# Earlier requests for plain weight tiles, and gate blocks read during convolution output

## The chip, the cores and the metric

One NeuronCore of a Trainium2 chip runs the whole layer in one launch. The metric is the device time in microseconds, as the median of several runs, beside one execution taken by the hardware profiler.

## The reference

One block of a language model on 512 positions of width 1024, in float32: half a feed-forward layer, a mixer, half a feed-forward layer, each on an RMS-normalized input and added to it, and a last normalization.

```python
for l in range(DEPTH):                                  # DEPTH = 1
    x = x + 0.5 * swiglu(rmsnorm(x, norm_ffn1_g[l]), ffn1_w_gu[l], ffn1_w_down[l])
    x = x + hybrid_mixer(rmsnorm(x, norm_mix_g[l]), w_in[l], ...)
    x = x + 0.5 * swiglu(rmsnorm(x, norm_ffn2_g[l]), ffn2_w_gu[l], ffn2_w_down[l])
return rmsnorm(x, final_norm_g)

def hybrid_mixer(h, w_in, conv_w, ..., w_out_conv, w_out_gla, w_o):
    cb, cc, cu, q, k, v, g_lr, r, ga, gb = split(h @ w_in)
    y_conv = (cb * causal_short_conv(cc * cu, conv_w)) @ w_out_conv
    o = gated_linear_attention(q, k, v, decay(g_lr))    # 4 heads, chunks of 64
    y_gla = (normalized(o) * silu(r)) @ w_out_gla
    return (sigmoid(ga) * y_conv + sigmoid(gb) * y_gla) @ w_o
```

The change concerns `sigmoid(gb) * y_gla`, with `y_conv` just ahead of it, and the order in which weights are fetched.

## The kernel before, in words

**Layout.** Activations lie transposed, features on the 128 partitions, positions along the row: a tile of 128 x 512 is one block of features. Each float32 operand is split into a high part (`h`, a copy by ScalarE, L310) and a low part (`l`, a subtraction by VectorE, L311), and a product is three matmuls.

**Plain tiles and sets of block products.** All weight units are listed in `PLAN`, and the order in which TensorE takes them in `STEPS`. An entry is either plain (`p` is None: one weight tile and its matmuls, 24 of them with 512 columns) or one of the seven products of a set (`m1`, `p2`, `q6`, `p5`, `q7`, `p4`, `p3`), by which a 2 x 2 block product takes seven block multiplications instead of eight. One such step is 24 matmuls with 256 columns (L502); ScalarE copies the results of `m1`, `q6` and `q7` out of PSUM (L507), and the next product into that bank waits for the copy. A set takes five tiles of the ring `f`: four weight blocks, which SP's queue reads, and a sum; four more sums are formed in place by accumulating DMAs that POOL issues (L288).

**The order of the stages.** First feed-forward: plain tiles, sets, then the plain tiles of the down projection. Mixer: plain tiles for attention's inputs, then twelve sets (`MSETS`: gates `ga` and `gb`, convolution, `r`), with attention's heads woven between them; then convolution output (`w_out_conv`, eight plain tiles, about 719 to 763 us in the profile); then attention output (`w_out_gla`, two sets, 763 to 807 us); then `w_o`, plain. Second feed-forward: plain tiles, sets, sets of another shape (`wide_sets`), and the last plain tiles.

**Who asks for weights.** `Weights.take` issues the split of the step two ahead. `issue` first calls `fetch`, which asks for the plain tiles among the next `early` steps (5 in the feed-forward layers, 4 in the mixer) and stops at the first set step; the blocks of a set are asked for six steps before its `m1`. All of these are reads of 512 KB into the ring `f` of ten tiles, on SP's queue (L284).

**Gates.** The `ga` and `gb` blocks of the mixer's input product go to DRAM when they are made. `gate(name, d, l, t)` reads a block back (L1307 for a whole tile of `ga`, L1309 for a half of two tiles of `gb`, 256 KB either way) and applies the sigmoid in place (ScalarE, L1311). Convolution output reads one `ga` tile for each of its eight tiles. Attention output reads four `gb` blocks for each of its sets, inside `gla_done`, into four work tiles of attention, `E`, `M`, `KS` and `EX`; both sets use these tiles. `E`, `M`, `KS` and `QS` are also used in convolution output's first four tiles, to spread the norms of the four heads (L1330, L1333). `vt[1]` are four tiles of the same shape that hold the values `v` of heads 2 and 3.

**What sets the order.** The text gives each instruction a priority; the framework's planner orders the instructions of each engine and queue with it, by its own estimate of durations, and starts an instruction ahead of others when its inputs and its tile are free. Tiles of a ring are given out in the order of the text. On the chip each queue then runs in that fixed order and waits for what isn't ready.

Of the kernel before, what the change touches and what calls it, by code (L numbers as in the profile page):

```python
# [102 lines left out]
STEPS = []  # L103
# [81 lines left out]
def block_kernel(ctx: ExitStack, tc: tile.TileContext, xT, vecs, gf, gup, wgl, wts, out):  # L185
# [21 lines left out]
    def tile_of(pool, shape, dtype=F32):  # L207
        cnt[0] += 1
        return pools[pool].tile(shape, dtype, tag=pool, name=f"{pool}{cnt[0]}")

    def T(dtype=F32):
        return tile_of("tp", [P, S], dtype)
# [31 lines left out]
    class Weights:  # L244
# [26 lines left out]
        def fetch(self, at):  # L271

            for n, p in STEPS[at : min(at + self.early, self.end)]:
                if p is None and n not in self.raw:
                    self.raw[n] = self.dma(n)
                elif p is not None:
                    break

        def dma(self, n):
# [62 lines left out]
    def mm_single(mat, kt, col, ah, al):  # L342
        o = MM()
        for u in single(mat, kt, col):
            h, l = W.take(u)
            for i in range(u[2]):
                k = u[1] + i
                mm3(o, h[:, i * P : (i + 1) * P], l[:, i * P : (i + 1) * P],
                    ah[k], al[k], k == 0, k == kt - 1)
        return o  # L350
# [124 lines left out]
    def mul(out_, a, b, eng=None):  # L475
        (eng or nc.vector).tensor_tensor(out=out_, in0=a, in1=b, op=ALU.mult)
# [390 lines left out]
    def mixer(norm, nxt):  # L867
# [13 lines left out]
        def two(i):  # L881
            return flat(i).rearrange("p (e t) -> p e t", e=2)
# [3 lines left out]
        vt = [[V0[t // 2][:, t % 2] for t in range(NTB)],  # L886
              [tile_of("v", [P, S]) for _ in range(NTB)]]

        def G_tile(i, dtype=F32):
            cnt[0] += 1  # L890
            return pools["g"].tile([P, S], dtype, tag=f"g{i}", name=f"g{i}_{cnt[0]}")
# [93 lines left out]
        E, M, KS, EX, QS = (G_tile(i) for i in range(5))  # L985
# [180 lines left out]
        def pair(t):  # L1166
            return t.rearrange("p (e t) -> p e t", t=HW)

        def half(l):
            return slice(l * HW, (l + 1) * HW)  # L1170
# [19 lines left out]
        def finish_late():  # L1190
            while late:
                late.pop(0)()
# [38 lines left out]
        def quarter(s, p):  # L1231

            bank, v = s.bank, s.v
            if p not in ("p2", "q7", "p3"):
                return None
            t = T()
            if p == "q7":
                nc.vector.scalar_tensor_tensor(out=t, in0=bank["c"], scalar=-1.0, in1=v["q7"],  # L1238
                                               op0=ALU.mult, op1=ALU.subtract)
            else:  # L1240
                nc.vector.tensor_tensor(out=t, in0=bank["a" if p == "p2" else "c"],
                                        in1=v["m1" if p == "p2" else "q6"], op=ALU.add)
            return t
# [49 lines left out]
        def split_pair(v):  # L1293
            h, l = (tile_of("op", [P, 2, S], F32R) for _ in range(2))
            nc.scalar.copy(h, v)
            nc.vector.tensor_tensor(out=l, in0=v, in1=h.bitcast(F32), op=ALU.subtract)
            return [(h[:, i], l[:, i]) for i in range(2)]
# [5 lines left out]
        def gate(name, d, l=None, t=None):  # L1303

            t = T() if t is None else t
            if l is None:
                nc.sync.dma_start(t, gates_d[name][d])  # L1307
            else:
                nc.sync.dma_start(pair(t), gates_d[name][d : d + 2, :, half(l)].rearrange(  # L1309
                    "e p t -> p e t"))  # L1310
            nc.scalar.activation(t, t, AF.Sigmoid)  # L1311
            return t
# [8 lines left out]
        Of = OB[0].rearrange("p h e t -> p (h e) t")  # L1321
        oo = Operands(lambda j, l: Of[:, 4 * j : 4 * j + 4, half(l)])
        AT = {3: "m1", 4: "p2", 6: "p5"}
        for d in range(KD):
            t = gate("ga", d)
            yp = mm_single("w_out_conv", KD, d * P, c_h, c_l)
            mul(m[d], yp, t)
            if d < HEADS:
                tr, orow = (E, M) if d % 2 else (KS, QS)
                nc.vector.tensor_copy(  # L1330
                    tr.rearrange("p (b c) -> p b c", c=32),
                    r64[:, 16 * d : 16 * (d + 1)].unsqueeze(2).to_broadcast([P, 16, 32]))
                nc.vector.transpose(orow, tr)  # L1333
                mul(O[d], O[d], orow.unsqueeze(1).to_broadcast([P, 2, S]))
            if d in AT:
                oo.make(AT[d])
        oo.sum("q6")
        m_h, m_l = [None] * KD, [None] * KD

        def gla_done(i):  # L1340
            sg = {}

            def done(s, p):
                if not (i == 1 and p in ("q6", "p5", "q7")):
                    finish_late()
                if p == "m1":
                    sg[0, 0] = gate("gb", 4 * i, 0, E)
                if p == "p5":
                    sg[1, 1] = gate("gb", 4 * i + 2, 1, M)
                    sg[1, 0] = gate("gb", 4 * i + 2, 0, KS)  # L1350
                if p == "p4":
                    sg[0, 1] = gate("gb", 4 * i, 1, EX)
                if p not in ("p2", "q7", "p4", "p3"):
                    return
                a, l = int(p in ("p4", "q7")), int(p in ("q7", "p3"))
                d = 4 * i + 2 * a
                g = sg[a, l]
                if p == "p4":
                    nc.vector.scalar_tensor_tensor(out=g, in0=s.bank["b"], scalar=-1.0, in1=g,
                                                   op0=ALU.mult, op1=ALU.mult)  # L1360
                else:
                    mul(g, quarter(s, p), g)
                y = two(d // 2)
                nc.vector.tensor_tensor(out=y[:, :, half(l)], in0=y[:, :, half(l)], in1=pair(g),
                                        op=ALU.add)
                if p in ("p4", "p3"):
                    def f():
                        for j, (b, c) in enumerate(split_pair(y)):
                            m_h[d + j], m_l[d + j] = b, c
                    late.append(f)  # L1370
            return done

        def reload():
            XS.append(big("X2"))
            x[:] = [XS[-1][:, k] for k in range(KD)]
            for k in range(KD):
                nc.gpsimd.dma_start(x[k], xs[k])

        run_sets(lambda i: Set(oo, gla_done(i)), hooks={(0, "p3"): [reload]})
        finish_late()  # L1380

# [24 lines left out]
    with phase("small2", f=10, tp=6, v=4, qk=2, g=1, y=4, small=1):  # L1406
        W.phase(4, 5)
        n2 = Norm(V_G2)
        mixer(nm, n2)
# [46 lines left out]
```

## Time and profile before

| | us |
|---|---|
| median of 3 runs | 1209.31 (1205.89 to 1211.93) |
| profiled execution | 1207.32 |
| its span, first to last instruction | 1205.6 |
| TensorE busy in it | 1187.8 (99%) |
| VectorE, ScalarE, POOL busy | 840.7, 612.1, 130.0 |
| read from HBM, written to it | 124.55 MB, 8.39 MB |

In rows of a timeline stand the start and the duration in us, the engine, the line, the operation and its tiles (out<-in), and in brackets the idle time of the engine before it with what ended it. In rows of waits stand the total, how often, and the longest. In rows of windows stand the stretch, its length, and for each engine the busy time with the count, then the granted TensorE clock, the share of the DMA engines and GB/s. In rows of the chain stand start, duration and what the end of the program hung on at that time.

### The profile page before, as it was taken

The numbers are of one execution on the slowest core, as the hardware profiler recorded it, in microseconds if no ns is written. First come the engines' busy times: TensorE is split into PE (matmuls) and PEld (weight loads), VectorE is DVE, ScalarE is ACT, GpSimd is POOL, SyncE is SP. The second block draws the span as 40 slices with busy tenths as digits, with TensorE's granted clock in tenths as the row PEclk, the third lists the DMA queues.
The fourth block names the chain that finished last, engine by engine and source line by source line (L and its number), as shares of the span: only waits on it lengthen the run. The fifth ranks groups of instructions, "written<-read, shape, count | busy, mean of one in ns | idle before, by whom it ended". The sixth has DMA issues, their size and how long they took to land.

```text
span 1205.6 us, 19145 instructions
## 1 busy us (share of the span) xinstructions
PE 1187.8 (99%) x7834; PEld 1092.1 (91%) x7834; DVE 840.7 (70%) x990; ACT 612.1 (51%) x762; POOL 130.0 (11%) x155
## 2 busy tenths in 40 slices
PE   9999999999999999999999999999999999999987
PEld 8899999988888889999999998898889999997776
DVE  7976666732277765868688687586597656589865
ACT  6555455532254465646554575454355455466453
POOL 0011111000010001101011100200001111113420
PEclk9999999999999999999999999999999999999999
DMA  9477777531162325767777756752447777757711
GB/s 349 95 200 189 178 187 186 167 105 53 52 241 92 88 70 150 213 171 186 194 184 176 192 182 183 208 149 93 161 99 194 189 175 177 183 143 197 161 50 70
DMA packets 59496, 190.81 MB, mean 158 GB/s; under 512 B 6576, under 2 KB 12848, under 8 KB 59408
## 3 DMA queue, kind: packets, MB, share of 16 engines
q1 hardware_dynamic: 37936, 124.27, 29.6%
q0 software_dynamic: 16832, 60.83, 27.3%
q10 hardware_dynamic: 4640, 4.49, 1.2%
q8 instruction: 61, 1.00, 0.3%
q14 instruction: 27, 0.22, 0.1%
HBM read 124.55 MB, written 8.39 MB: 110 GB/s over the span
## 4 chain that ended last, share of the span: by engine, by line
PE 89%; DVE 4%; DMA 3%; issue 2%; ACT 1%; POOL 0%; SPq 0%; DVEq 0%; ACTq 0%; POOLq 0%
PE mm L502 50%; PE mm L362 7%; PE mm L340 6%; PE mm L338 6%; PE mm L339 6%; DVE wl L311 2%; DMA f<-f 1%; PE mm L380 1%; PE mm L381 1%; PE mm L379 1%; DMA g<-gb 1%; DMA f<-wts 1%; PE aux L340 1%; PE aux L338 1%; PE aux L339 1%
## 5 line engine op out<-in xcount | busy, mean ns | idle before, releaser
L502 PE MATMUL mm<-op,wh 128*128 128x256 f32 x3584 | 649.9, 284 | 3.3 <-ACT tp L507 3.3
L310 ACT CAST wh<-f 128x1024 fp32r<-128x1024 f32 (+1 forms) x325 | 339.6, 1046 | 483.6 <-PE mm L502 225.2
L311 DVE TENSOR_TENSOR wl<-f,wh 128x1024 fp32r<-128x1024 f32 (+1 forms) x325 | 400.4, 1235 | 242.0 <-ACT wh L310 230.2
L502 PEld LDWEIGHTS mm<-op,wh 128*128 128x128 f32 x3584 | 560.2, 192 | 4.9 <-ACT tp L507 3.9
L502 PE MATMUL mm<-op,wl 128*128 128x256 f32 x1792 | 507.9, 284 | 0.0
L502 PEld LDWEIGHTS mm<-op,wl 128*128 128x128 f32 x1792 | 344.0, 192 | 0.1
L288 POOL DMA_DIRECT2D f<-f x108 | 93.3, 869 | 847.0 <-DVE wl L311 470.1
L340 PE MATMUL mm<-op,wl 128*128 128x512 f32 x324 | 126.4, 390 | 0.1
L338 PE MATMUL mm<-op,wh 128*128 128x512 f32 x324 | 126.5, 390 | 0.0
L339 PE MATMUL mm<-op,wh 128*128 128x512 f32 x324 | 126.1, 389 | 0.0
L340 PEld LDWEIGHTS mm<-op,wl 128*128 128x128 f32 x324 | 60.8, 188 | 13.2 <-DVE wl L311 0.5
L339 PEld LDWEIGHTS mm<-op,wh 128*128 128x128 f32 x324 | 60.8, 188 | 12.6
L338 PEld LDWEIGHTS mm<-op,wh 128*128 128x128 f32 x324 | 60.8, 188 | 12.4
L362 PE MATMUL mm<-op,wh 128*128 128x512 f32 x256 | 63.5, 390 | 0.3 <-DVE op L413 0.3
L362 PEld LDWEIGHTS mm<-op,wh 128*128 128x128 f32 x256 | 47.9, 188 | 10.6 <-ACT acc L422 0.4
L507 ACT COPY tp<-mm 128x512 f32<-128x512 f32 x96 | 55.8, 581 | 1.2 <-DVE tp L1238 1.0
L747 PE MATMUL mm<-wh,op 128*128 128x512 f32 x112 | 44.4, 398 | 4.1 <-ACT wh L310 2.4
L749 PE MATMUL mm<-wl,op 128*128 128x512 f32 x112 | 45.0, 401 | 2.1 <-DVE wl L311 2.0
L297 DVE TENSOR_TENSOR f<-f,f 128x1024 f32<-128x1024 f32 x36 | 44.0, 1221 | 1.8 <-DMA f<-f 1.0
L751 PE MATMUL mm<-wh,op 128*128 128x512 f32 x112 | 44.2, 395 | 0.0
L551 DVE TENSOR_TENSOR op<-hidw,op 128x1024 fp32r<-128x1024 f32 x28 | 36.0, 1297 | 1.3 <-ACT op L550 1.3
L550 ACT CAST op<-hidw 128x1024 fp32r<-128x1024 f32 x28 | 29.1, 1047 | 11.0 <-DVE hidw L597 4.0
(270 smaller groups left out, 1157.6 us busy)
## 6 DMA issues: line engine op xcount, KB each, us to landing
f<-wts SPq DMA_DIRECT2D x219, 512.0 KB, 4.3
f<-f POOLq DMA_DIRECT2D x108, 512.0 KB, 5.0
X<-xT SPq DMA_DIRECT2D x8, 256.0 KB, 4.9
xs<-X POOLq DMA_DIRECT2D x8, 256.0 KB, 5.4
ga<-tp ACTq DMA_DIRECT2D x8, 256.0 KB, 3.9
gb<-tp ACTq DMA_DIRECT2D x8, 256.0 KB, 4.1
g<-gb SPq DMA_DIRECT2D x8, 256.0 KB, 3.8
tp<-ga SPq DMA_DIRECT2D x8, 256.0 KB, 4.8
```

The source lines that it names most:

```text
L288: nc.gpsimd.dma_start(out_, a, accum_op=ALU.add)
L310: nc.scalar.copy(h[:, :w], raw[:, :w])
L311: nc.vector.tensor_tensor(out=l[:, :w], in0=raw[:, :w], in1=h[:, :w].bitcast(F32), op=ALU.subtract)
L338: nc.tensor.matmul(o, wh, ah, start=first, stop=False)
L339: nc.tensor.matmul(o, wh, al, start=False, stop=False)
L340: nc.tensor.matmul(o, wl, ah, start=False, stop=last)
L362: nc.tensor.matmul(o[c], w[:, s : s + P], a[k], start=k == 0 and j == 0, stop=k == kt - 1 and j == 2)
L502: nc.tensor.matmul(to, ww[:, s], aa[:, t], start=fresh and k == 0 and e == 0 and j == 0, stop=k == 3 and j == 2, skip_group_check=True)
L507: nc.scalar.copy(v, o)
L747: nc.tensor.matmul(o[t], bh[:, s], wh, start=fresh and k == 0, stop=False, skip_group_check=True)
L749: nc.tensor.matmul(o[t], bh[:, s], wl, start=False, stop=False, skip_group_check=True)
L751: nc.tensor.matmul(o[t], bl[:, s], wh, start=False, stop=k == 3, skip_group_check=True)
```

## The change

Two edits. In `fetch`, the search for plain tiles no longer stops at a set step when the step being issued is itself one of a set: it passes over the rest of the set and asks for the plain tiles behind it, up to `early` steps ahead. Where the step being issued is plain, it stops as before.

In the mixer, the eight `gb` reads and sigmoids leave `gla_done`. `early_gate` is called once for each tile of convolution output: for tiles 0 to 3 it reads set 0's four blocks into the tiles `vt[1]`, for tiles 4 to 7 set 1's four into `E`, `M`, `KS` and `EX`. `gla_done` takes them from the table `gb`.

```diff
@@ fetch
                 if p is None and n not in self.raw:
                     self.raw[n] = self.dma(n)
-                elif p is not None:
+                elif p is not None and STEPS[at][1] is None:
                     break
@@ mixer
         AT = {3: "m1", 4: "p2", 6: "p5"}
+        gb = {}
+
+        def early_gate(i, a, l, t):
+            gb[i, a, l] = gate("gb", 4 * i + 2 * a, l, t)
+
         for d in range(KD):
             t = gate("ga", d)
             yp = mm_single("w_out_conv", KD, d * P, c_h, c_l)
...
             if d in AT:
                 oo.make(AT[d])
+            if d < 4:
+                early_gate(0, d % 2, d // 2, vt[1][d])
+            else:
+                early_gate(1, d % 2, (d - 4) // 2, (E, M, KS, EX)[d - 4])
...
         def gla_done(i):
-            sg = {}
-
             def done(s, p):
                 if not (i == 1 and p in ("q6", "p5", "q7")):
                     finish_late()
-                if p == "m1":
-                    sg[0, 0] = gate("gb", 4 * i, 0, E)
-                if p == "p5":
-                    sg[1, 1] = gate("gb", 4 * i + 2, 1, M)
-                    sg[1, 0] = gate("gb", 4 * i + 2, 0, KS)
-                if p == "p4":
-                    sg[0, 1] = gate("gb", 4 * i, 1, EX)
                 if p not in ("p2", "q7", "p4", "p3"):
                     return
                 a, l = int(p in ("p4", "q7")), int(p in ("q7", "p3"))
                 d = 4 * i + 2 * a
-                g = sg[a, l]
+                g = gb[i, a, l]
```

## The prediction

> **What bounds the kernel now.** I read the page first, then who waits for whom on TensorE, then the chain of waits around the two stages that the change touches, then the timelines there.
>
> ```profile
> span 1205.6 us, 19145 instructions
> PE 1187.8 (99%) x7834; PEld 1092.1 (91%) x7834; DVE 840.7 (70%) x990; ACT 612.1 (51%) x762; POOL 130.0 (11%) x155
> PE mm L502 <- ACT tp L507: 3.3, 3, 1.8
> PE mm L747 <- ACT wh L310: 2.4, 1, 2.4
> PE mm L749 <- DVE wl L311: 2.0, 4, 0.9
> ```
>
> TensorE is busy for 1187.8 of 1205.6 us, so 17.8 us is all that a better order of transfers could give, and some of that is the start and the end. The waits of TensorE say where the rest lies: 3.3 us in the block products (L502) for ScalarE's copy out of PSUM (L507), and 4.4 us in the last stage (L747, L749). The chain shows what stands behind the first of these.
>
> ```profile
> 762.96 5.77 PE mm L502 x48
> ...
> 771.37 0.61 DVE y L1364
> ...
> 772.00 7.88 DMA g<-gb
> ...
> 781.52 0.49 ACT tp L507
> ...
> 782.06 24.79 PE mm L502 x192
> 806.85 0.23 PE mm L362
> 779.96 0.63 ACT L1311 ACTIVATE g<-g 128x512 f32<-128x512 f32 x1 [4.53 <-DMA g<-gb]
> 782.65 1.05 ACT L310 CAST wh<-f 128x1024 fp32r<-128x1024 f32 x1 [0.65 <-DMA f<-f]
> 782.06 0.50 PE L502 MATMUL mm<-op,wh 128*128 128x256 f32 x2 [1.84 <-ACT tp L507]
> 894.41 25.92 PE mm L502 x216
> ```
>
> This is attention output (762.96 to 806.85). Tile E serves both sets of products: set 0's use ends at 771.98 (L1364), only then may set 1's gate block be read into it, and the read takes 7.88 us. ScalarE works in order; the sigmoid (L1311) stands at the head of its queue and holds it for 4.53 us, with a weight split (L310) and the copy L507 behind it. TensorE needs that copy and stands idle for 1.84 us.
>
> **The change, part by part.**
>
> *Gate blocks read earlier.* It removes all eight reads and sigmoids from the block products of attention output and puts them into the loop of convolution output, one per tile. Set 0's four go to the V tiles, set 1's to E, M, KS, EX, so no read waits for the other set's use any more. The stage holds 14 steps of 24 products. Undisturbed, a product takes 25.92 / 216 = 0.120 us (row at 894.41), so the stage needs 336 x 0.120 = 40.3 us; it took 806.85 - 762.96 = 43.9. The 3.6 us between are the gap (782.06 - 779.95, less one product: about 2.0) and what follows it:
>
> ```profile
> 779.95 0.28 PE L502 MATMUL mm<-op,wl 128*128 128x256 f32 x1
> 713.00:717.00 4.00, 4.00 (x33) 4.00 (x34) 3.72 (x5) 3.97 (x5) 0.00 (x0) 1.00 0.81 244
> 782.10:786.00 3.90, 3.90 (x21) 3.90 (x22) 3.80 (x5) 1.53 (x2) 0.00 (x0) 0.59 0.47 143
> 1150.70:1155.00 4.30, 4.23 (x12) 3.26 (x13) 4.30 (x5) 3.05 (x5) 0.00 (x0) 0.60 0.33 114
> ```
>
> After the gap the granted clock was 0.59 for 3.9 us: 3.9 x 0.41 = 1.6 us lost. So a gap here can cost nearly twice itself. Not each one does: after the gap that ended at 713.0 the clock stayed at 1.00. Term: -3.6 us, with both parts gone, since neither the read nor the sigmoid is left in the stage.
>
> [...]
>
> What is late next there? The rows at 782.65 and below: the accumulating DMA for the sixth step's weights.
>
> ```profile
> 774.11 0.89 POOL L288 DMA_DIRECT2D f<-f  x1 [2.92 <-DVE wl L311]
> L311 DVE TENSOR_TENSOR wl<-f,wh 128x1024 fp32r<-128x1024 f32 (+1 forms) x325 | 400.4, 1235 | 242.0 <-ACT wh L310 230.2
> ```
>
> Issued at 774.11, it ended ScalarE's wait at 782.65. Without the stall that split (1.05, then VectorE's 1.23) ends by 784.9; its step would begin at 779.95 + 2 x 2.88 = 785.7. So it hides with 0.8 us to spare, and one 256 KB read less competes with it. If it were late, the stage would lose that lateness again: 0 to 1 us; I take 0.
>
> *Where the reads go.* The planner does not keep to the place in the text: a read goes out when its tile is free.
>
> ```profile
> 576.86 0.39 SPq L1309 DMA_DIRECT2D g<-gb  x1
> 577.84 1.28 ACT L1311 ACT_TABLE_LOAD   x1
> 580.57 0.63 ACT L1311 ACTIVATE g<-g 128x512 f32<-128x512 f32 x1 [1.45 <-DMA g<-gb]
> 595.83 0.39 PE L1092 MATMUL aux<-g,stt 128*128 128x128 f32 x2
> 603.14 0.62 ACT L389 CAST tp<-g 128x512 fp32r<-128x512 f32 x1 [0.21 <-issue]
> 604.91 0.44 PE L1105 MATMUL aux<-tp,ones_r 128*128 128x512 f32 x1
> 606.54 1.28 ACT L467 ACT_TABLE_LOAD   x1
> 590.00:612.00 22.00, 22.00 (x185) 21.91 (x185) 14.28 (x21) 12.91 (x17) 2.43 (x3) 1.00 0.78 193
> DMA to landing us min/median/max: 2.6/3.8/7.9
> ```
>
> The first gate read of set 0 (tile EX) went out at 576.86, 186 us before its stage. The V tiles are free when the last attention head's output is done (L1089 and L1092, about 596), so I expect the four new reads there, on SP's queue between weight reads, and EX's fifth one only after gate set 1 has been written (past 603). E, KS and M keep their places near 704 to 724, now with set 1's blocks. ScalarE gets 4 x 0.63 = 2.5 us and one or two table loads of 1.28 into a stretch where it is busy for 12.91 of 22 us: room for that. What can hurt is the wait in front of the first of them, as ScalarE then holds L389, and TensorE's L1105 follows that cast within 1.8 us. Bounds: 0, as in the row at 580.57, where ScalarE waited 1.45 us and TensorE nothing; or as much as the stage at 780, 3.6 us with the clock. The row at 580.57 is the nearest (same tile size, same neighbours): I take 0. VectorE's work is the same; SP issues eight reads as before (0.39 us each), and they cannot block weight reads for longer than the wait for one tile.
>
> *The stall at 711.* It also hangs on a gate read:
>
> ```profile
> 704.01 0.63 DVE g L1333
> ...
> 704.69 5.79 DMA g<-gb
> ...
> 710.55 1.28 ACT L1311
> 711.84 0.63 ACT g L1311
> 712.47 0.48 ACT tp L507
> ...
> 713.00 4.33 PE mm L502 x34
> ```
>
> The read into E waits for the transpose L1333, which is not moved, and stands in front of L507 again. Only the block read is another one. I take 0; gone, it would give up to 1.3 us, and 1 us more could be lost if ScalarE's order there gets worse.
>
> *Plain tiles asked for earlier.* The lookup now passes over up to four (mixer: three) block products to the plain tiles behind them. Between the old place and the new one no other tile of the ring f is taken: the last set's loads lie at least 15 steps and its sum at least 12 steps before the end. So the ring is given out in the same order, and a weight read is bound by its slot:
>
> ```profile
> SPq L284 <- DVE wl L311: 30.4, 9, 5.5
> SPq L284 <- DMA f<-f: 30.2, 2, 27.8
> 1147.28 1.04 ACT L310 CAST op<-f 128x1024 fp32r<-128x1024 f32 x1 [7.23 <-DMA f<-wts]
> ```
>
> The first is SP's wait from 676 to 720 (before convolution output), the second from 1100 to 1155 (before the last plain tiles): the queue stands waiting for a split or an accumulating DMA to release a slot. Asked for sooner, it waits sooner. Term: 0; below by nothing, above by the stall at 1147 that the last row belongs to.
>
> **Sum.** 1205.6 - 3.6 = 1202.0 us of span; the profiled execution took 1207.32, 1.7 more than its span, so 1203.7. The median of the runs, 1209.31, lies 2.0 above that execution; against it: 1205.7.
>
> **The rivals.**
>
> 1. *The wait moves to 596 to 606 and costs more than it did (slower).* Worst read to land 7.9 us: 596.3 + 7.9 = 604.2; then a table load and four sigmoids (3.8) before L389: 608.0; L1105 follows 1.8 us behind as now, at 609.8 instead of 604.9. With the clock's 1.6 that is +6.5 - 3.6 = +2.9 us: 1212.2. It decides from a delay of 2.0 us at L1105 (3.6 with the clock); it passes 1215.4 only if EX's own read, right behind, costs as much again. For it: DMA share 0.78 there. Against: the row at 580.57. [...]
>
> 2. *The last stage's stall goes too (faster).* If asking earlier does free the plain tiles at 1141, or the planner writes another order there, TensorE wins the idle and the slow clock of 1140 to 1155: 10.7 - 7.48 = 3.2 idle and 4.3 x 0.40 = 1.7.
>
> ```profile
> 1140.00:1150.70 10.70, 7.48 (x32) 5.62 (x30) 4.38 (x5) 3.47 (x5) 0.00 (x0) 1.00 0.68 250
> ```
>
> That is -4.9: 1200.8. For it: ScalarE takes a tile of the plain part (op) ahead of block weights there, an order that hangs on small differences. Against: the slots above.
>
> 3. *Nothing moves.* The planner puts the V tiles' sigmoids late, so that the copy waits as before: 1209.3. Against: the reads of EX and E went out as soon as they could.
>
> **How the numbers follow.** This kernel's runs scatter from 1205.89 to 1211.93, so 0.5% (6 us) is about the least that can be told from no change. Forecast (3.6 us or up to 1.3 more): 0.50. Rival 1: 0.26, of which 0.08 above 1215.4. Rival 2: 0.14. Rival 3: 0.10. Faster than 1203.3: rival 2 and a part (0.07) of the forecast, 0.21. Slower than 1215.4: 0.08 and a little for an order that I don't foresee, 0.10. Same: 0.69. The range reaches from rival 2, 1200, to rival 1, 1212.5; the forecast's own is 1203 to 1208.
>
> **What would show it.** Right: no L1309 read between 762 and 806; products of that stage in 40.3 us at clock 1.00; four L1309 reads near 596; SP's weight reads in the same order with the same waits for slots; the gap at 711 still there. Wrong: an idle row of TensorE in front of L1105 or L502 between 596 and 612 put down to ScalarE; a sigmoid still in attention output; weight reads that go out with no wait before convolution output; another order at 1141.

## The result, and the profile after

| | before | after |
|---|---|---|
| median of the timed runs, us | 1209.1 (14 runs, 1203.4 to 1211.9) | 1212.28 (14 runs, 1209.2 to 1215.3) |
| ratio after / before | | 1.0029, 95% interval 1.0017 to 1.0041 |
| profiled execution, its span, us | 1207.32, 1205.6 | 1212.55, 1210.8 |
| TensorE busy, us | 1187.8 | 1189.7 |

The change costs about 3.5 us (0.0029 x 1209). The interval of the ratio leaves out 1, so this is a small loss, where a gain of 3.6 us was forecast: the sign is wrong. The median lies 0.1 us from rival 1's 1212.2, but much of that nearness is luck: rival 1 reckoned with one loss and one gain, while the table below has four more steps, +1.9 us together, and the medians moved by 2.0 us less than the profiled spans.

Who waits for whom on TensorE after the change (total us, how often, longest):

```profile
PE aux L1104 <- ACT tp L389: 4.2, 1, 4.2
PE mm L502 <- ACT tp L507: 2.9, 3, 2.1
PE mm L749 <- DVE wl L311: 1.9, 4, 0.9
PE mm L747 <- ACT wh L310: 1.8, 1, 1.8
```

The first row is new: a wait of 4.2 us in front of L1104, near 604. The second was expected to shrink by the 1.8 us of the gap at 780, and it kept a wait of 2.1 us. To see what each costs, I subtract the start of the same matmul in the two traces; where the lag changes, time was lost or won. TensorE's order is the same in both but for L1104 and its partner L1105, which stand ten products (1.2 us) earlier after the change.

| place (time before) | lag there, us | step | what stands there |
|---|---|---|---|
| 57 to 603 | 0.63 | +0.63 | an early difference at 57 |
| 603 to 614 | 7.36 | +6.73 | new gap in front of L1104 (4.24 us), then slow clock (0.50) |
| 711 to 714 | 6.72 | -0.64 | the gap at 711 has become smaller |
| 780 to 787 | 3.17 | -3.55 | the gap at 780 and its slow clock are gone (1.00 from 780 to 787) |
| 798 to 806 | 6.97 | +3.80 | new gap in front of L502 (2.05 us), then slow clock (0.50) |
| 1145 to 1157 | 5.07 | -1.90 | the last stage's gap is shorter (1.8 us for 2.4), with a clock of 1.00 behind it where it was 0.60 |

The predicted gain of the gap at 780 is there, in this pair of profiles at its predicted size. Two losses have come, one of them named by rival 1, the other named nowhere. The first one, in the timeline after the change:

```profile
593.03 0.39 SPq L1309 DMA_DIRECT2D g<-gb  x1
595.54 0.38 SPq L1309 DMA_DIRECT2D v<-gb  x1
596.08 0.36 SPq L284 DMA_DIRECT2D f<-wts  x1
596.54 3.34 SPq L1309 DMA_DIRECT2D v<-gb  x3
```

```profile
598.08 1.28 ACT L1311 ACT_TABLE_LOAD   x1
599.37 0.63 ACT L1311 ACTIVATE g<-g 128x512 f32<-128x512 f32 x1
599.91 1.03 ACT L310 CAST wh<-f 128x1024 fp32r<-128x1024 f32 x1
602.14 0.63 ACT L1311 ACTIVATE v<-v 128x512 f32<-128x512 f32 x1 [1.20 <-DMA v<-gb]
605.44 2.03 ACT L1311 ACTIVATE v<-v 128x512 f32<-128x512 f32 x3 [2.67 <-DMA v<-gb]
606.93 0.37 ACTq L1263 DMA_DIRECT2D gb<-tp  x1
607.38 0.60 ACT L389 CAST tp<-g 128x512 fp32r<-128x512 f32 x1
```

```profile
608.04 0.79 PE L1104 MATMUL aux<-tp,ones_r 128*128 128x512 f32 x1 [4.24 <-ACT tp L389]
```

The same matmul before the change, without a wait:

```profile
604.20 0.40 PE L1104 MATMUL aux<-tp,ones_r 128*128 128x512 f32 x1
```

The four reads into the V tiles go out between 595.54 and 599.88, as predicted. They land late: the trace gives 6.6, 7.9 and 8.9 us from issue to landing as least, median and longest for these four. ScalarE waits 1.20 and 2.67 us at the head of its queue, then does the sigmoids, and the cast L389 that TensorE needs starts at 607.38, not at 603.14 as before. What follows is read from the windows (stretch, its length, busy time and count of TensorE, weight load, VectorE, ScalarE, POOL; granted clock, DMA share, GB/s):

```profile
590.00:603.40 13.40, 13.40 (x117) 13.40 (x115) 7.76 (x9) 8.91 (x12) 1.72 (x2) 1.00 0.94 236
603.40:607.90 4.50, 0.40 (x4) 0.19 (x2) 0.00 (x0) 2.31 (x5) 0.00 (x0) 0.83 0.61 224
607.90:612.00 4.10, 3.96 (x16) 3.77 (x17) 2.55 (x4) 1.03 (x2) 0.00 (x0) 0.50 0.17 60
612.00:616.00 4.00, 4.00 (x31) 4.00 (x30) 2.04 (x4) 3.24 (x5) 0.86 (x1) 0.85 0.42 133
806.10:810.00 3.90, 3.69 (x22) 3.70 (x23) 3.90 (x7) 1.10 (x2) 0.00 (x0) 0.71 0.38 132
```

The gap of 4.24 us is followed by a clock of 0.50 for 4.1 us and of 0.85 for 4.0 us: 4.1 x 0.50 + 4.0 x 0.15 = 2.65 us more. 4.24 + 2.65 = 6.89, against the step of 6.73 in the table.

The second loss, on ScalarE, first after the change and then before it:

```profile
799.42 1.04 ACT L310 CAST wh<-f 128x1024 fp32r<-128x1024 f32 x1
804.72 1.04 ACT L310 CAST wh<-f 128x1024 fp32r<-128x1024 f32 x1 [4.26 <-DMA f<-f]
805.67 0.58 ACT L507 COPY tp<-mm 128x512 f32<-128x512 f32 x1
```

```profile
797.41 0.63 ACT L1311 ACTIVATE g<-g 128x512 f32<-128x512 f32 x1 [1.06 <-DMA g<-gb]
798.25 0.59 ACT L507 COPY tp<-mm 128x512 f32<-128x512 f32 x1 [0.21 <-PE mm L502]
800.02 2.03 ACT L310 CAST wh<-f 128x1024 fp32r<-128x1024 f32 x2 [1.19 <-DMA f<-f]
```

Before, a gate's sigmoid and then the copy of step `q7` (L507) stood ahead of the weight split that waits for an accumulating DMA. With the sigmoid gone from the stage, the planner puts that split ahead of the copy. The split waits 4.26 us for its DMA, the copy stands behind it, and TensorE waits for the copy, from 804 on:

```profile
806.30 0.51 PE L502 MATMUL mm<-op,wh 128*128 128x256 f32 x2 [2.05 <-ACT tp L507]
```

Behind it the clock is 0.71 in the window from 806.10 to 810.00. The slow stretch outlasts that window: the clock is 0.50 from 807.76 to 811.17, which costs 1.7 us.

### The profile page after: what moved, and what is told of

It is laid out like the page before. It is cut to its first block, busy times and chain, and to the rows that moved or that the text cites. A ratio compares the mean times of both kernels' runs of the same rounds, so it can differ in the third digit from the quotient of the medians.

```text
span 1210.8 us, 19135 instructions
## 1 busy us (share of the span) xinstructions
PE 1189.7 (98%) x7834; PEld 1093.7 (90%) x7834; DVE 840.5 (69%) x990; ACT 611.6 (51%) x762; POOL 129.9 (11%) x155
## 5 line engine op out<-in xcount | busy, mean ns | idle before, releaser
L502 PE MATMUL mm<-op,wh 128*128 128x256 f32 x3584 | 651.8, 284 | 2.9 <-ACT tp L507 2.9
L502 PEld LDWEIGHTS mm<-op,wh 128*128 128x128 f32 x3584 | 561.8, 193 | 4.6 <-ACT tp L507 3.5
L502 PE MATMUL mm<-op,wl 128*128 128x256 f32 x1792 | 508.9, 284 | 0.2 <-DVE wl L311 0.2
L502 PEld LDWEIGHTS mm<-op,wl 128*128 128x128 f32 x1792 | 345.0, 193 | 0.6 <-DVE wl L311 0.4
L507 ACT COPY tp<-mm 128x512 f32<-128x512 f32 x96 | 55.8, 581 | 1.0 <-DVE tp L1238 1.0
L747 PE MATMUL mm<-wh,op 128*128 128x512 f32 x112 | 43.8, 392 | 3.6 <-ACT wh L310 1.8
```

The lines of the kernel that those rows point to most:

```text
L502: nc.tensor.matmul(to, ww[:, s], aa[:, t], start=fresh and k == 0 and e == 0 and j == 0, stop=k == 3 and j == 2, skip_group_check=True)
L507: nc.scalar.copy(v, o)
```

## The experiments

**The theories.** A: the first loss is ScalarE's queue, held by the V tiles' sigmoids in front of L389. B: it is the traffic of the early reads. C: the other edit, in `fetch`, costs something. Later D: the second loss is the `q7` copy behind the weight split; E: taking that away only uncovers a wait for the same weights two steps later. Ratios are to the kernel before, on the same chip.

**The fetch edit alone.** `Weights.fetch` as in the change, the gates as before.

> The lookup of plain tiles alone; gates as before. Theory A (the loss is ScalarE held by the sigmoids of the four V tiles, about 602 to 607, in front of L389): nothing of that is here; time as before, ratio 0.998 to 1.002, no gap at L1104, the gap of 1.84 us in front of L502 at 780 and the one of 1.1 at 712 stand. Theory C (the earlier requests fill the ring f differently and cost): about 3 us slower than before, weight reads in another order or with other waits.

Measured: 1208.62, ratio 1.0015 (1.0001 to 1.0030). The compiled program holds the same instructions in the same order on every engine and queue as the kernel before, tile names aside. So the edit does nothing here, and C is out; the 0.15% is what two programs of the same order differ by in these runs, though its interval just leaves out 1. A ratio this near to 1 is therefore not read as a gain or a loss below. Its profile also shows that the gap which the change was to remove has no fixed length. TensorE's row at that place:

```profile
786.00 0.80 PE L502 MATMUL mm<-op,wh 128*128 128x256 f32 x2 [4.58 <-ACT tp L507]
```

4.58 us here, where the profile before had 1.84. The gap of 1.1 us at 712, which was expected to stand, isn't there.

**The gates alone.** The gates as in the change, `fetch` as before.

> The gate reads alone; lookup as before. Theory A: as the changed kernel, ratio 1.002 to 1.004, gap of about 4.2 us in front of L1104 near 603.5 and about 2.0 us near 804, no gap at 780. Theory C: as before, 1209.

Measured: 1210.61, ratio 1.0039 (1.0024 to 1.0055); the program has the order of the changed kernel. Its waits on TensorE:

```profile
PE aux L1104 <- ACT tp L389: 4.2, 1, 4.2
...
PE mm L502 <- ACT tp L507: 1.7, 2, 1.3
```

The gap near 804 is 1.3 us, where about 2.0 was expected. The whole effect of the change is in the gates.

**The reads pinned to their place in the text.** Each read is made to wait for its own tile of convolution output:

```diff
         def early_gate(i, a, l, t):
+            nc.vector.tensor_copy(t[:, 0:1], m[d][:, 0:1])
             gb[i, a, l] = gate("gb", 4 * i + 2 * a, l, t)
```

> The changed kernel, and each of the eight gate tiles gets one column of convolution output's tile d written into it first, so that its read and sigmoid can't start before that tile. Theory A: no gap at L1104; none at 712, as no gate read stands in front of L507 there (-1.4); none at 780 (-3.5); the one at 804 stays (+3.4 with the slow clock): 1207 to 1208.5, ratio 0.997 to 1.000. Theory B (the additional 256 KB reads delay other transfers wherever they are put): gaps of 1 to 4 us between 725 and 770, time 1210 or more.

Measured: 1206.3, ratio 0.9992 (0.9979 to 1.0004). The reads go out between 729.1 and 766.5; no gap near 603, none at 712 or 780. What stays is the second loss:

```profile
PE mm L502 <- ACT tp L507: 2.5, 2, 2.1
```

Reads and sigmoids have both left the stretch near 600, so A and B are not told apart yet.

**Reads early, sigmoids late.** The reads go out as in the change; only the sigmoids wait, by a bias of zeros worked out from the convolution output's tile.

```diff
-            nc.scalar.activation(t, t, AF.Sigmoid)
+            if after is None:
+                nc.scalar.activation(t, t, AF.Sigmoid)
+            else:
+                nc.scalar.activation(t, t, AF.Sigmoid, bias=after)
...
-            gb[i, a, l] = gate("gb", 4 * i + 2 * a, l, t)
+            z = zero[:, 4 * i + d % 4 : 4 * i + d % 4 + 1]
+            nc.vector.tensor_scalar(out=z, in0=m[d][:, 0:1], scalar1=0.0, scalar2=None,
+                                    op0=ALU.mult)
+            gb[i, a, l] = gate("gb", 4 * i + 2 * a, l, t, z)
```

> The changed kernel with its reads where they are, but the eight sigmoids take a bias of zero made from convolution output's tile d, so that they can't run before it. Theory A: the reads still land at 596 to 607, yet no gap at L1104 and no gate in front of L507 at 712; the gap at 804 stays: 1207 to 1208.5. Theory B (the traffic of the reads delays the weights): a gap of 2 us or more stays between 596 and 612, put down to a weight split, and the time stays at 1211 to 1212.

Measured: 1205.31, ratio 0.9990 (0.9979 to 1.0002). SP's queue, ScalarE and the windows in this kernel:

```profile
596.85 0.37 SPq L1309 DMA_DIRECT2D v<-gb  x1
...
597.84 3.34 SPq L1309 DMA_DIRECT2D v<-gb  x3
```

```profile
603.83 1.05 ACT L310 CAST wh<-f 128x1024 fp32r<-128x1024 f32 x1 [1.83 <-PE mm L502]
604.68 0.37 ACTq L1263 DMA_DIRECT2D gb<-tp  x1
605.08 0.62 ACT L389 CAST tp<-g 128x512 fp32r<-128x512 f32 x1 [0.21 <-issue]
```

```profile
590.00:603.40 13.40, 13.40 (x116) 13.40 (x116) 8.11 (x8) 7.19 (x11) 1.72 (x2) 1.00 0.91 223
603.40:612.00 8.60, 8.60 (x72) 8.51 (x71) 6.32 (x10) 5.79 (x7) 0.86 (x1) 1.00 0.86 292
```

The same reads at the same place, landing as slowly (6.6, 7.7 and 8.7 us), with the DMA share at 0.91 and 0.86, and TensorE is busy in the whole of 590 to 612 at full clock. Nothing waits for these tiles before 730, so their landing costs nothing. B is out; A stands. One thing moves along with the sigmoids: L1104 is back at its old place in TensorE's order, ten products later than in the changed kernel, so this run doesn't part the wait from the order; the next one does. The second loss stays, with a gap of 3.05 us in front of the same product. Between the changed kernel and this one lies 1.0029 - 0.9990 = 0.0039, or 4.7 us.

**One cast taken out of the held queue.** The changed kernel, with the cast L389 of head 3 given to VectorE; the sigmoids stay where they hold ScalarE, and TensorE's order is that of the changed kernel.

```diff
-            sh, sl = split(E)
+            if h == 3:
+                sh, sl = T(F32R), T(F32R)
+                nc.vector.tensor_copy(sh, E)
+                nc.vector.tensor_tensor(out=sl, in0=E, in1=sh.bitcast(F32), op=ALU.subtract)
+            else:
+                sh, sl = split(E)
```

> The changed kernel, with head 3's rounding of E (tp790, L389) given to VectorE; the four sigmoids stay at the head of ScalarE's queue, and the weight split (607.89 in the changed kernel) stays behind them. Theory A in its narrow form (TensorE's only tie to the held queue is that cast): the gap of 4.24 us in front of L1104 is gone; the next product that needs ScalarE is 40 products on (about 609.3), when the split is just done, so at most 1 us comes back there. About 6 us less than the changed kernel: 1206, ratio to before 0.997 to 1.000; the gap near 804 stays. Theory A in its wide form (the whole queue is late, splits too): the gap comes back in front of L502 near 609 with 2 to 4 us, and the time stays at 1209 to 1212. Rival B (reads slow down all transfers): the gap stays in some form, 1212.

Measured: 1206.44, ratio 0.9985 (0.9972 to 0.9998): 0.0044, or 5.3 us, off the changed kernel. ScalarE and then VectorE there:

```profile
604.70 2.05 ACT L1316 ACTIVATE v<-v 128x512 f32<-128x512 f32 x3 [2.67 <-DMA v<-gb]
606.20 0.37 ACTq L1268 DMA_DIRECT2D gb<-tp  x1
606.65 1.98 ACT L310 CAST wh<-f 128x1024 fp32r<-128x1024 f32 x2
608.54 0.58 ACT L507 COPY tp<-mm 128x512 f32<-128x512 f32 x1
```

```profile
602.52 0.42 DVE L1104 CAST tp<-g 128x512 fp32r<-128x512 f32 x1
602.98 0.69 DVE L1105 TENSOR_TENSOR tp<-g,tp 128x512 fp32r<-128x512 f32 x1
```

ScalarE is held by the same 2.67 us, and the gap in front of the matmul on the cast is gone; what comes back is 0.83 us at 609 for a copy (L507) that is late by the same queue, as theory A's narrow form expects. The hold itself is nearly free: the 6.7 us came of one instruction behind it whose result TensorE needed soon.

**The second loss.** In three kernels the copy of step `q7` in the second set goes to VectorE (`self.vector` is `("q7",)` for that set and empty else), and the order on TensorE, SP and POOL stays as it was:

```diff
-                nc.scalar.copy(v, o)
+                if p in self.vector:
+                    nc.vector.tensor_copy(v, o)
+                else:
+                    nc.scalar.copy(v, o)
```

On the changed kernel:

> The changed kernel, with the q7 copy of attention output's second set given to VectorE and nothing else changed. Theory D: the gap of 2.05 us near 804 and the slow clock behind it (3.9 us at 0.71) go, the gap in front of L1104 (4.2 us) stays: 1212.3 - 3.2 = about 1209, ratio to before 1.000 to 1.002. Rival E: a gap of 1 to 2 us at a weight two steps later, 1210.5 to 1212, ratio 1.002 to 1.004.

Measured: 1208.77, ratio 1.0007 (0.9995 to 1.0019), 2.7 us less than the changed kernel; the wait in front of the matmul behind L389 stays at 3.8 us, the gap at 804 is gone.

On the pinned kernel:

> The pinned kernel (each gate read waits for its own tile of convolution output) with one copy more taken off ScalarE: the copy of step q7 of the second set in attention output (L507) goes to VectorE. Theory D (the gap of 2.1 us near 797 in the pinned kernel is this copy standing behind a weight split that waits for the accumulating DMA): no gap of TensorE in attention output, some 2 to 3.5 us less than the pinned kernel: about 1203.5, ratio to before 0.996 to 0.998. Rival E (the step behind needs the same accumulated weights, so the wait only shows two steps later): a gap of 1 to 2 us in front of L502 at a weight (wh or wl), and about 1205.5 to 1206.5, ratio 0.998 to 1.000.

Measured: 1203.74, ratio 0.9967 (0.9954 to 0.9980), 3.0 us less. D expected no gap at all; 0.27 and 0.70 us are left, in front of products that wait for `wl`, and that is all there is of what E expected.

On the kernel with early reads and late sigmoids:

> The kernel with early reads and late sigmoids (each sigmoid waits for its tile of convolution output), with the q7 copy given to VectorE. Theories A and D together: no gap in front of L1104, none in attention output over 0.5 us; 1205.3 less 2 to 3: about 1202.5, ratio to before 0.995 to 0.998, and so the fastest of all. Rival E: a gap at a weight two steps behind the copy, 1204.5 to 1205.5, ratio 0.998 to 0.999.

Measured: 1202.14 (1200.35 to 1203.91), ratio 0.9957 (0.9940 to 0.9973): the lowest of all, below both kernels of the case by 5.2 and 8.7 us; its interval overlaps that of the pinned kernel just above. All of TensorE's waits that the trace lists (lines from `Set` on stand 4 lower here), and two windows:

```profile
PE mm L753 <- DVE wl L311: 1.9, 4, 0.9
PE mm L751 <- ACT wh L310: 1.8, 1, 1.8
PE mm L751 <- ACT tp L760: 1.7, 1, 1.7
PE aux L229 <- POOL ones L226: 1.1, 1, 1.1
PE mm L503 <- ACT tp L511: 0.3, 1, 0.3
```

```profile
590.00:612.00 22.00, 22.00 (x185) 21.91 (x185) 14.61 (x21) 12.84 (x17) 2.58 (x3) 1.00 0.91 242
755.00:800.00 45.00, 45.00 (x351) 43.87 (x351) 33.88 (x39) 25.09 (x28) 6.93 (x11) 1.00 0.65 188
```

Both stages run without a gap and at clock 1.00. D holds: the gap went in all three kernels, and E's wait came in none but the pinned one, and there smaller. What is left lies in the last stage and at the start.

## Why the prediction was wrong

**The step that failed first is "Where the reads go".** It had the reads, the tiles and the place right (four reads near 596, ScalarE held, L389 and the matmul behind it late) and took 0 between bounds of 0 and 3.6 us. Measured: +6.7. Three things went wrong in it.

- The row that set the value told the wrong thing. At 580.57 ScalarE waited 1.45 us and TensorE nothing, and I took tile size and neighbours as the likeness. What decides is the slack of the instruction behind the wait, that is, how long its result can be late before another engine stands idle. I counted 1.8 us, from the cast at 603.14 to L1105 at 604.91, but L1105 is the second matmul on this cast. The first, L1104, started at 604.20, and the cast had ended at 603.76: 0.4 us of slack. After the change the cast ended 3.6 us later (607.98 against 603.76, less the lag of 0.63), and the new order asked for it 1.2 us earlier: 3.6 - 0.4 + 1.2 = 4.4, and the gap is 4.24. The cast taken off ScalarE shows the tie: same hold, same order on TensorE, no gap in front of that matmul.
- The length of the hold was taken from one read alone (landed in 3.7 us). The four new ones, close together, needed 6.6 to 8.9 us. The load on the DMA engines alone doesn't tell them apart: their share was 1.02 while that one read was under way (576.8 to 580.6 before) and 0.94 over 595.5 to 607 after. Why these take longer stays open. Rival 1 used 7.9 and came out at 608.0 for the cast; it started at 607.38.
- The upper bound was too low. It was the stage at 780 (1.84 us and its clock of 0.59); the gap here was longer, and so was the slow clock, 2.65 us in place of 1.6. Rival 1's +6.5 came within 0.2 of the measured step, in part by luck: its delay of 4.9 us was too long and its 1.6 us of slow clock too short, and the two errors nearly cancel.

EX's read, which I expected past 603, went out at 593.03, ahead of the last two writes of gate blocks (L1263, at 595.26 and 606.93), so it waited for neither; its sigmoid (599.37) cost nothing, as ScalarE waited again behind it (1.20 us).

**"Gate blocks read earlier"** was right in its first half: the gap at 780 and its slow clock are gone, 3.55 us against 3.6. That the size fits is partly luck, as the same order had a gap of 4.58 us in another execution. The second step that failed is its clause on what is late next there, 0 taken between bounds of 0 and 1 us. It named the sixth step's weights and missed the order itself: in the changed kernel a split that waits for an accumulating DMA goes ahead of the copy of `q7`, for +3.8 us. So the whole stage, which was to become 3.6 us shorter, became 0.25 us longer. I had asked which wait ends last in the old order, and not what the removal does to the order. The three kernels with the copy on VectorE show that this copy behind that split is the cause of the gap. That the planner chose this order because the sigmoid had left is my reading of two orders; its estimates were not looked at.

**"The stall at 711"**: 0 taken, -0.64 measured, inside its bounds. It need not come of the change: the fetch edit alone, with the order of before, has no wait there. **"Plain tiles asked for earlier"**: 0 taken and 0 found, as the order of every queue is the same with that edit alone; the slots of the ring bound the reads already (before, SP's queue waited 30.4 us for splits from 676 to 720, and 30.2 us for accumulating DMAs from 1100 to 1155).

**Rival 2's gain** shows in part (-1.9 in the last stage), but not by its cause: with the order of before, the fetch edit alone has 1.7 us in that row (L747 for `wh`) against 2.4, so the gap's length varies from one execution to the next. I don't count it as an effect of the change.

The sum by the measured steps: 0.63 + 6.73 - 0.64 - 3.55 + 3.80 - 1.90 = 5.07 us, and the spans differ by 1210.8 - 1205.6 = 5.2. The medians differ by less, 3.2. One profile of each kernel can't settle why, but it fits that the removed gap was short in the profile of before (1.84, and 4.58 in another execution of the same order), and that the new one at 804 is 1.3 in the kernel with the gates alone and 2.05 here.

## What to carry to other kernels

Before an operation that waits for a transfer is moved into an in-order queue, look at what stands behind it there and how soon that result is needed: the wait cost here what it exceeded this slack by (the cast 3.6 us later, 0.4 us of slack, and the result asked for 1.2 us earlier: 4.4, with a gap of 4.24), and a nearby wait of 1.45 us of ScalarE said nothing about it. Count the slack to the first instruction that needs the result. Start the transfer early and let the operation on it be issued late: here the reads in flight cost nothing (with late sigmoids TensorE was busy for 22.00 of 22.00 us while they landed in 6.6 to 8.7 us), and the engine that waited for them did. Where a planner orders the queues, compare the order around the place that an instruction leaves, too: its gap may be filled by something that waits longer (here a split with a wait of 4.26 us, where the sigmoid had waited 1.06).

## What the runs showed of the hardware

The length of a gap does not settle the clock after it. Of the gaps in front of one and the same product, 2.13 us in the pinned kernel and 3.05 with late sigmoids were followed by full clock (1.00); 2.05 in the changed kernel and 2.80 in the kernel with the cast on VectorE were followed by a slow stretch (windows at 0.71 and 0.59). The windows behind these four gaps, in this order:

```profile
799.70:803.70 4.00, 3.88 (x32) 3.89 (x33) 4.00 (x7) 1.84 (x3) 0.00 (x0) 1.00 0.38 131
801.20:805.00 3.80, 3.72 (x31) 3.72 (x32) 3.80 (x7) 1.63 (x3) 0.00 (x0) 1.00 0.41 138
806.10:810.00 3.90, 3.69 (x22) 3.70 (x23) 3.90 (x7) 1.10 (x2) 0.00 (x0) 0.71 0.38 132
800.30:804.30 4.00, 3.90 (x20) 3.90 (x21) 4.00 (x7) 0.99 (x2) 0.00 (x0) 0.59 0.39 131
```

Gaps of nearly the same length differ too: behind 1.84 us at 782.06 before the change the clock fell to 0.50, and behind 1.76 us in the last stage after the change (ended at 1155.61) it stayed at 1.00. The slow stretches around the gaps of the two profiles, two before the change and two after it:

```profile
782.80:786.21 3.41, 3.41 (x19) 3.41 (x18) 3.10 (x4) 1.39 (x2) 0.00 (x0) 0.50 0.56 165
1151.44:1154.85 3.41, 3.41 (x10) 2.55 (x9) 3.41 (x4) 2.22 (x3) 0.00 (x0) 0.50 0.24 97
606.38:613.20 6.82, 5.16 (x22) 4.97 (x23) 2.66 (x5) 3.64 (x6) 0.00 (x0) 0.50 0.17 50
807.76:811.17 3.41, 3.41 (x19) 3.41 (x18) 3.41 (x6) 0.68 (x1) 0.00 (x0) 0.50 0.45 154
```

Windows of 3.5 to 4.4 us on both sides of each show a clock of 1.00. Three of these stretches last 3.41 us; the one of 6.82 us begins inside the longest gap, 4.24 us up to 608.04. No run here moves a gap on purpose, so what decides whether a slow stretch follows a gap was not shown.
